# Gate and up products of a SwiGLU layer: k-tiles outside and both token tiles inside, in place of one token tile after the other

## Chip, cores, metric

One core of one Trainium2 chip. The metric is the device time of one launch in microseconds (us). The kernel before takes 947.87 us, the median of 3 runs (947.01 to 948.15). TensorE is called PE below, VectorE DVE, ScalarE ACT, GpSimd POOL, SyncE SP.

## What is computed

A two-layer encoder over 256 tokens of width 1024, all in float32. Each layer is a feed-forward half step, a mixer and a second feed-forward half step, each of them behind an RMSNorm:

```
def swiglu(h, w_gate, w_up, w_down):
    return (jax.nn.silu(h @ w_gate) * (h @ w_up)) @ w_down

for layer in range(DEPTH):                       # DEPTH = 2
    x = x + 0.5 * swiglu(rms_norm(x, ffn1_norm[layer]), ...)
    x = x + mixer(rms_norm(x, mix_norm[layer]))  # attention; even and odd layers differ
    x = x + 0.5 * swiglu(rms_norm(x, ffn2_norm[layer]), ...)
return rms_norm(x, final_norm)
```

The four feed-forward steps (width 2816) are the stages 0, 2, 3 and 5 of the kernel; the mixers are stages 1 and 4. The change touches the four feed-forward stages.

## The kernel before

**A product.** Weights come from memory as float32 into tiles `raw` (SP issues the transfers). Each is split in two: `hi`, which ACT copies in a rounded format (L476), and `lo`, the rest, which DVE subtracts (L479). The method `mm` (L459) makes one 128 x 512 product out of three matmuls (L468 to L470): `h*hi`, `h*lo`, `l*hi`, where (h, l) are the two parts of the transposed activations (`th`, `tl`). A piece is one k-tile of 128 rows; a split has two of them, and each piece is used by two products, one for each of the two token tiles (`tt` 0 and 1).

**What sets the order.** The order of every engine's instructions is the order in which the Python code writes them. After every product `mm` calls `tick` (L273). A tick counts down the waits of small tasks (Python generators that write the next ACT or DVE instruction when their wait is over) and adds `self.rate` to a budget `due`. When the budget and `room` (seven `hi`/`lo` pairs may live, L286) allow it, the next split is written. A split that a product needs and that isn't there is written on the spot. All engines then run their rows strictly in this order, and a row that waits holds up everything behind it on its engine.

**Chunks.** `ffn` (L656) goes through five chunks of 512 columns, numbered 0 to 4, and one mixed chunk of 256. There are two kinds. A plain chunk takes 8 gate pieces and 8 up pieces. Gate: `project` (L599) makes all 8 products of token tile 0 in one PSUM bank, then all 8 of token tile 1 in another; behind each a task `silu` (L667) is started, which reads the bank on ACT. Up: the same again, with a task `glu` (L671) behind each, which reads the up bank on DVE (L674) and multiplies. Six ticks later `transposed` (L677) begins: ACT splits the result in two 16-bit planes (L553), SP issues a transposing transfer (L555), and 16 ticks later ACT puts the planes together again (L557) and ACT and DVE split the outcome (`g_h`, `g_l`), or make sums of it (`quarters`).

The other kind, `seven_gates` (L753), makes gate and up of a chunk with seven products in place of eight. It is chunk 2 in stages 0 and 5, and chunks 1 and 3 in stages 2 and 3: six in all. It begins with 8 plain products (16 where two pairs of k-tiles are plain) into the banks M00, M10, M01, M11, with token tiles 0 and 1 in turn; then the seven-product part begins in the banks M1, M5, M7 and M6. At its end ACT copies M1 (`copy`, L764, written `glu<-pj`), DVE reads M00 together with that copy (L785, `silu<-s`), and further DVE rows read M1's companions: L800 reads M01, L804 M10, L806 M5.

**Banks.** PSUM has eight: two with the tag `pj`, three with `s`, one `o`, two `tp` (L126). A tag's banks are given out in turn, and the first matmul into a bank waits until the last reader of what was there before has ended. A plain chunk takes `s, s` for gate and `pj, pj` for up; behind a seven-product chunk it takes `pj, s` for gate and `s, pj` for up (L861). So the first gate bank behind a seven-product chunk is M1's, the second one M00's; the second up bank is M5's. M1, the first `pj` bank of a seven-product chunk, is the one that the chunk before gave to up of token tile 0, where that chunk took `pj, pj` for up; in chunk 3 of stages 2 and 3 it is M01 that takes over the bank of up of token tile 0, an `s` bank there.

## Time and profile before

| what | before |
|---|---|
| time, median of 3 runs | 947.87 us |
| profiled execution: its time | 949.13 us |
| profiled execution: span from first to last instruction | 947.3 us |
| PE busy | 924.9 us, 98% of the span, 4399 matmuls |
| DVE busy | 789.6 us, 83% |
| ACT busy | 678.6 us, 72% |
| POOL busy | 90.8 us, 10% |
| transfers | 183.16 MB, mean 193 GB/s |
| mean granted TensorE clock | 0.996 |

PE is busy in nearly every slice of the profile. Busy isn't the same as at its peak: a matmul of 128 x 512 is shown with some 0.39 us, while the next one begins 0.23 us after it. So what PE loses is read from the distance between the starts of two matmuls, and from idle time in the view of the waits. DVE and ACT make the splits that PE uses, and read the banks that PE fills.

### The profile page before, as it was taken

The page shows a single profiled execution, that of the slowest core. Times are in us where ns is not written, and L with a number is a line of the kernel's source. Part 1 is how long each engine was busy: PE and PEld are TensorE (multiplying, and loading weights), DVE is VectorE, ACT ScalarE, POOL GpSimd, SP SyncE. Part 2 cuts the span into 40 slices and gives each one's busy share as a digit, 9 for nine tenths or more (in the row PEclk, how much of TensorE's full clock was granted, in tenths as well). Part 3 has the DMA queues.
Part 4 walks back from the last instruction along what each step waited for, and adds up shares of the span by engine and source line. Part 5 has one row for each costly group of instructions (what it writes and reads, how often), then busy time and mean ns, then how long its engine had stood idle before and what let it go on. Part 6 is the DMA issues. An engine that isn't in the chain of part 4 may idle for free.

```text
span 947.3 us, 12407 instructions
## 1 busy us (share of the span) xinstructions
PE 924.9 (98%) x4399; PEld 755.3 (80%) x4399; DVE 789.6 (83%) x1228; ACT 678.6 (72%) x1091; POOL 90.8 (10%) x152
## 2 busy tenths in 40 slices
PE   9999999999999999999999999899999999999997
PEld 6887888877788788888888778688778788878886
DVE  6799788778879988798878887988777787988797
ACT  7687875568787687874757868647777587769753
POOL 1300000064410000000100000007030000000001
PEclk9999999999999999999999999999999999999999
DMA  8858986554236677867458677665444449489761
GB/s 297 274 170 243 248 226 215 176 155 102 93 110 189 214 213 230 264 192 266 148 151 250 173 256 208 219 221 159 147 134 134 134 151 271 116 275 256 186 222 45
DMA packets 129343, 183.16 MB, mean 193 GB/s; under 512 B 50688, under 2 KB 63744, under 8 KB 129280
## 3 DMA queue, kind: packets, MB, share of 16 engines
q1 hardware_dynamic: 128704, 181.58, 62.4%
q8 instruction: 34, 0.56, 0.2%
q10 hardware_dynamic: 576, 0.79, 0.2%
q14 instruction: 29, 0.24, 0.1%
HBM read 169.76 MB, written 1.05 MB: 180 GB/s over the span
## 4 chain that ended last, share of the span: by engine, by line
PE 72%; DVE 15%; ACT 6%; issue 4%; DMA 2%; POOL 0%; SPq 0%; POOLq 0%; ACTq 0%; DVEq 0%
PE s L469 10%; PE s L470 10%; PE s L468 10%; PE pj L468 9%; PE pj L469 9%; PE pj L470 9%; DVE lo L479 6%; PE o L470 2%; PE o L469 2%; PE o L468 2%; ACT hi L476 2%; PE o L1038 2%; DVE raw L394 1%; DVE two L394 1%; PE tp L1117 1%
## 5 line engine op out<-in xcount | busy, mean ns | idle before, releaser
L479 DVE TENSOR_TENSOR lo<-raw,hi 128x1024 fp32r<-128x1024 f32 (+1 forms) x372 | 376.2, 1030 | 83.6 <-ACT hi L476 81.9
L476 ACT ACTIVATE hi<-raw 128x1024 fp32r<-128x1024 f32 (+1 forms) x372 | 319.3, 889 | 54.5 <-PE s L470 16.7
L469 PE MATMUL s<-lo,th 128*128 128x512 f32 x373 | 145.9, 391 | 2.5 <-DVE lo L479 2.4
L468 PE MATMUL pj<-hi,th 128*128 128x512 f32 x367 | 146.6, 399 | 1.3 <-ACT glu L764 1.3
L468 PE MATMUL s<-hi,th 128*128 128x512 f32 x373 | 146.2, 392 | 0.0
L470 PE MATMUL s<-hi,tl 128*128 128x512 f32 x373 | 145.6, 390 | 0.0
L469 PE MATMUL pj<-lo,th 128*128 128x512 f32 x367 | 143.5, 391 | 1.6 <-DVE lo L479 1.5
L470 PE MATMUL pj<-hi,tl 128*128 128x512 f32 x367 | 143.2, 390 | 0.0
L469 PEld LDWEIGHTS s<-lo,th 128*128 128x128 f32 x373 | 70.2, 188 | 18.2 <-DVE lo L479 4.0
L469 PEld LDWEIGHTS pj<-lo,th 128*128 128x128 f32 x367 | 69.1, 188 | 16.0 <-DVE lo L479 3.3
L470 PEld LDWEIGHTS s<-hi,tl 128*128 128x128 f32 x373 | 70.2, 188 | 14.5
L468 PEld LDWEIGHTS s<-hi,th 128*128 128x128 f32 x373 | 70.1, 188 | 14.2
L468 PEld LDWEIGHTS pj<-hi,th 128*128 128x128 f32 x367 | 69.0, 188 | 15.6 <-ACT glu L764 1.7
L470 PEld LDWEIGHTS pj<-hi,tl 128*128 128x128 f32 x367 | 68.9, 188 | 14.5
L488 POOL TENSOR_TENSOR rstd<-var,mhalf 128x1 f32<-128x1 f32 (+2 forms) x16 | 17.1, 1070 | 601.8 <-ACT th L509 321.5
L557 ACT COPY turned<-glu 128x1024 uint16<-128x1024 uint16 (+1 forms) x48 | 60.2, 1254 | 6.1 <-DMA glu<-turned 6.1
L470 PE MATMUL s<-hi,g_l 128*128 128x512 f32 (+1 forms) x131 | 51.5, 393 | 3.6 <-DVE g_l L479 3.6
L553 ACT COPY turned<-glu 128x1024 uint16<-128x1024 uint16 (+1 forms) x48 | 46.2, 963 | 8.9 <-DVE glu L674 6.7
L468 PE MATMUL s<-hi,g_h 128*128 128x512 f32 (+1 forms) x131 | 52.0, 397 | 0.0
L469 PE MATMUL s<-lo,g_h 128*128 128x512 f32 (+1 forms) x131 | 51.3, 392 | 0.0
L476 ACT ACTIVATE shi<-two 128x1024 fp32r<-128x1024 f32 x30 | 31.7, 1057 | 26.2 <-DVE two L394 26.1
L476 ACT ACTIVATE shi<-raw 128x1024 fp32r<-128x1024 f32 x30 | 31.7, 1056 | 23.9 <-PE s L470 13.0
(483 smaller groups left out, 1685.3 us busy)
## 6 DMA issues: line engine op xcount, KB each, us to landing
raw<-in_ffn_w_down SPq DMA_DIRECT2D x44, 1024.0 KB, 5.4
raw<-in_ffn_w_up SPq DMA_DIRECT2D x28, 1024.0 KB, 5.3
raw<-in_ffn_w_gate SPq DMA_DIRECT2D x26, 1024.0 KB, 5.2
raw<-in_ffn_w_gate SPq DMA_DIRECT2D x35, 512.0 KB, 4.1
raw<-in_ffn_w_up SPq DMA_DIRECT2D x32, 512.0 KB, 5.2
raw<-in_odd_w_qkv SPq DMA_DIRECT2D x12, 1024.0 KB, 5.4
raw<-in_even_w_in SPq DMA_DIRECT2D x4, 1024.0 KB, 5.1
raw<-in_even_w_out SPq DMA_DIRECT2D x8, 512.0 KB, 5.7
```

The costliest lines, as they stand in the source:

```text
L394: add = lambda o, x, y: self.nc.vector.tensor_tensor(o, x, y, op=ALU.add)
L468: mm(ps, h, wh, start=first, stop=False)
L469: mm(ps, h, wl, start=False, stop=False)
L470: mm(ps, l, wh, start=False, stop=last)
L476: self.nc.scalar.activation(hi, src, AF.Copy)
L479: self.nc.vector.tensor_tensor(lo, src, hi.bitcast(F32), op=ALU.subtract)
L488: nc.gpsimd.tensor_tensor(r[:, :n], v[:, :n], self.mhalf[:, :n], op=ALU.pow)
L553: self.nc.scalar.copy(planes.rearrange("p (h c) -> p h c", h=2), back.rearrange("p (c h) -> p h c", h=2))
L557: self.nc.scalar.copy(planes.rearrange("p (c h) -> p h c", h=2), back.rearrange("p (h c) -> p h c", h=2))
L1038: self.nc.tensor.matmul(O[64 * s : 64 * s + 64, i * P : i * P + P], v(b0 + i, s, kc), pT[s][:, i, kc, :], start=(kc == 0), stop=(kc == 1),)
L1117: nc.tensor.transpose(tb[:, o : o + P], p[:, i, kc * P : kc * P + P], self.ident)
```

## The change

```
     def project(self, hT, pieces, tag):
...
+    def project_both(self, pieces, tags):
+        ps = [self.bank(tag) for tag in tags]
+        n = len(pieces)
+        for k in range(n):
+            for tt in range(NT):
+                self.mm(ps[tt], self.now.hT[tt][k], pieces[k], k == 0, k == n - 1)
+        return ps
...
             if self.now.n + ci == 0:
                 both = self.first_gates(G)
+            if ci:
+                both = self.project_both(G, tags[:NT])
             for tt in range(NT):
-                g = both[tt] if self.now.n + ci == 0 else self.project(self.ready(tt), G, tags[tt])
+                g = both[tt] if self.now.n + ci == 0 or ci else self.project(self.ready(tt), G, tags[tt])
                 S.append(self.t([P, 512], "silu", 2))
                 self.start(silu(tt, w, g, S[tt]))
             U = self.take(KD)
+            last = ci + 1 == len(FF_CHUNKS)
+            if not last:
+                both = self.project_both(U, tags[NT:])
             for tt in range(NT):
-                u = self.project(self.now.hT[tt], U, tags[NT + tt])
+                u = self.project(self.now.hT[tt], U, tags[NT + tt]) if last else both[tt]
                 tasks.append(self.start(glu(tt, f0, w, u, S[tt])))
```

Gate of the plain chunks from chunk 1 on (10 of them) and up of all plain chunks but chunk 4 (10 too, and chunk 0 among them) now take each piece for both token tiles in turn. The number of products and of ticks is the same. Both banks are in use from the first two products on, and both `silu`, or both `glu`, are started behind the sixteenth product; before, the first was started behind the eighth. A piece is first used later (but for the first one) and is done with sooner.

Three places show what moved. The names end in numbers that count the tiles; between the two kernels they differ by a few.

The first is PE at the start of chunk 4 of stage 2, behind a seven-product chunk. Here `pj_3760` is the bank of gate for token tile 0 (`th_2918` its activations), and `s_3761` that for token tile 1 (`th_3004`). Before:

```order
L468 MATMUL pj_3760<-hi_3697,th_2918 128x512
L469 MATMUL pj_3760<-lo_3698,th_2918 128x512
L470 MATMUL pj_3760<-hi_3697,tl_2919 128x512
L468 MATMUL pj_3760<-hi_3697,th_2918 128x512
L469 MATMUL pj_3760<-lo_3698,th_2918 128x512
L470 MATMUL pj_3760<-hi_3697,tl_2919 128x512
```

And with the change:

```order
L468 MATMUL pj_3760<-hi_3690,th_2918 128x512
L469 MATMUL pj_3760<-lo_3691,th_2918 128x512
L470 MATMUL pj_3760<-hi_3690,tl_2919 128x512
L468 MATMUL s_3761<-hi_3690,th_3004 128x512
L469 MATMUL s_3761<-lo_3691,th_3004 128x512
L470 MATMUL s_3761<-hi_3690,tl_3005 128x512
```

The bank of token tile 1 is taken at the fourth matmul of the chunk; before, it was taken at the twenty-fifth.

The second is ACT at the same place, in the last part of the seven-product chunk 3 of stage 2. `turned` are results of up of chunk 2 (two token tiles); `glu<-pj` is the copy of M1. Before:

```order
L553 COPY turned_3628<-glu_3581 128x1024
L476 ACTIVATE shi_3630<-two_3610 128x1024
L557 COPY turned_3568<-glu_3525 128x2x512
L698 ACTIVATE quarters_3670<-turned_3568 128x256
L476 ACTIVATE g_8_h_3672<-turned_3568 128x512
L476 ACTIVATE shi_3688<-raw_3481 128x1024
L476 ACTIVATE hi_3697<-raw_3537 128x1024
L476 ACTIVATE hi_3704<-raw_3537 128x1024
L557 COPY turned_3628<-glu_3581 128x2x512
L701 ACTIVATE quarters_3670<-turned_3628 128x128
L764 ACTIVATE glu_3718<-pj_3663 128x512
L476 ACTIVATE hi_3720<-raw_3600 128x1024
```

And with the change:

```order
L476 ACTIVATE shi_3681<-raw_3479 128x1024
L476 ACTIVATE hi_3690<-raw_3520 128x1024
L476 ACTIVATE hi_3697<-raw_3520 128x1024
L557 COPY turned_3629<-glu_3580 128x2x512
L557 COPY turned_3631<-glu_3582 128x2x512
L706 ACTIVATE quarters_3711<-turned_3629 128x256
L476 ACTIVATE g_8_h_3713<-turned_3629 128x512
L709 ACTIVATE quarters_3711<-turned_3631 128x128
L772 ACTIVATE glu_3717<-pj_3662 128x512
L476 ACTIVATE hi_3719<-raw_3591 128x1024
```

The three rows of token tile 0 (`COPY turned`, `quarters`, `g_8_h`) stood ahead of the last `shi`; now they stand behind it and behind two `hi`, right ahead of the copy of M1.

The third is DVE at the end of chunk 2 of stage 2, where up ends and the seven-product chunk begins. `glu<-s` reads the up bank of token tile 0, `glu<-pj` that of token tile 1. Before:

```order
L674 SCALAR_TENSOR_TENSOR glu_3525<-s_3488,rstd_2940,silu_3437 128x512
L479 TENSOR_TENSOR lo_3531<-raw_3409,hi_3530 128x1024
L479 TENSOR_TENSOR lo_3547<-raw_3455,hi_3546 128x512
L394 TENSOR_TENSOR two_3553<-raw_3455 128x1024
L394 TENSOR_TENSOR raw_3455<-two_3553,raw_3455 128x512
L394 TENSOR_TENSOR raw_3455<-raw_3455 128x512
L479 TENSOR_TENSOR g_4_l_3544<-turned_3446,g_4_h_3543 128x512
L479 TENSOR_TENSOR lo_3562<-raw_3455,hi_3561 128x1024
L674 SCALAR_TENSOR_TENSOR glu_3581<-pj_3521,rstd_3030,silu_3487 128x512
L479 TENSOR_TENSOR slo_3584<-two_3553,shi_3583 128x1024
```

And with the change:

```order
L479 TENSOR_TENSOR lo_3514<-raw_3410,hi_3513 128x1024
L479 TENSOR_TENSOR lo_3529<-raw_3445,hi_3528 128x512
L394 TENSOR_TENSOR two_3535<-raw_3445 128x1024
L394 TENSOR_TENSOR raw_3445<-two_3535,raw_3445 128x512
L394 TENSOR_TENSOR raw_3445<-raw_3445 128x512
L479 TENSOR_TENSOR lo_3553<-raw_3445,hi_3552 128x1024
L479 TENSOR_TENSOR g_4_l_3550<-turned_3451,g_4_h_3549 128x512
L479 TENSOR_TENSOR slo_3561<-two_3535,shi_3560 128x1024
L682 SCALAR_TENSOR_TENSOR glu_3580<-s_3487,rstd_2940,silu_3485 128x512
L682 SCALAR_TENSOR_TENSOR glu_3582<-pj_3488,rstd_3030,silu_3486 128x512
```

The reader of the first up bank went from the head of these rows to their end, and one `slo` more stands ahead of it.

## Prediction

> **What bounds the kernel now.** The busy times come first, then PE's waits.

> ```profile
> PE 924.9 (98%) x4399; PEld 755.3 (80%) x4399; DVE 789.6 (83%) x1228; ACT 678.6 (72%) x1091; POOL 90.8 (10%) x152
> ```

> ```profile
> PE s L470 <- DVE g_l L479: 3.6, 1, 3.6
> PE s L469 <- DVE lo L479: 2.4, 2, 2.0
> PE pj L469 <- DVE lo L479: 1.5, 2, 0.9
> ```

> PE is the bound: it idles 22.4 of 947.3 us, and its longest sum of waits for one thing is 3.6. So little can be won, and whatever makes PE wait once more is paid in full. The question is whether the new order makes it wait, and for whom.

> **What the change takes away.** A plain chunk before needs its four splits within 8 products; with the change within 16, so splits 2 to 4 are first used 6, 12 and 18 matmuls later. Where PE waited for a late `lo` of such a chunk, that wait goes: the third wait row above, 1.5 us, is the fourth split of gate in chunk 3 of stages 0 and 5. This one, in chunk 4 of stage 2, is of the same kind:

> ```profile
> 369.50 0.39 PE L468 MATMUL pj<-hi,th 128*128 128x512 f32 x1
> 369.87 0.50 PE L469 MATMUL pj<-lo,th 128*128 128x512 f32 x1
> ```

> The starts lie 0.37 us apart where 0.23 is usual. With a like one at the start of stage 0 and the slow restart behind each, I put all of this at **-2.5 us**. Matmuls, splits, transfers and their bytes are the same in number, so nothing else goes away.

> **What it adds: banks that are read late.** The second gate bank behind a seven-product chunk is M00's, and DVE's L785 reads it. Chunk 4 of stage 2, PE, then ACT, then DVE:

> ```profile
> 365.42 0.39 PE L468 MATMUL pj<-hi,th 128*128 128x512 f32 x1
> ...
> 366.10 0.39 PE L468 MATMUL pj<-hi,th 128*128 128x512 f32 x1
> ...
> 371.14 0.39 PE L468 MATMUL s<-hi,th 128*128 128x512 f32 x1
> ```

> ```profile
> 355.86 1.34 ACT L557 COPY turned<-glu 128x1024 uint16<-128x1024 uint16 x1
> 357.23 0.42 ACT L698 ACTIVATE quarters<-turned 128x256 f32<-128x256 f32 x1
> 357.55 0.62 ACT L476 ACTIVATE g_h<-turned 128x512 fp32r<-128x512 f32 x1
> 359.50 1.06 ACT L476 ACTIVATE shi<-raw 128x1024 fp32r<-128x1024 f32 x1 [1.33 <-PE pj L470]
> ...
> 363.97 0.58 ACT L764 ACTIVATE glu<-pj 128x512 f32<-128x512 f32 x1
> 364.45 1.05 ACT L476 ACTIVATE hi<-raw 128x1024 fp32r<-128x1024 f32 x1
> ```

> ```profile
> 365.53 1.23 DVE L479 TENSOR_TENSOR lo<-raw,hi 128x1024 fp32r<-128x1024 f32 x1 [1.43 <-ACT hi L476]
> 366.67 0.42 DVE L704 TENSOR_TENSOR quarters<-turned,quarters 128x256 f32<-128x256 f32 x1
> 367.00 0.69 DVE L785 TENSOR_TENSOR silu<-s,glu 128x512 f32<-128x512 f32 x1
> ```

> L785 ends at 367.69. Before, the second bank is wanted at 371.14, and nobody sees it. With the change it is wanted at 366.10, the fourth matmul of the chunk: 1.6 us short as it stands. And L785 comes later. ACT's three rows from 355.86 to 358.17 go behind the two `hi` after 359.50 and ahead of the copy of M1; the `shi` at 359.50 waits for PE, so ACT can't begin it sooner, and the gap of 1.33 us that they leave stays empty. So the copy of M1 ends 2.3 us later (366.9, past the gate's start at 365.42), the `hi` behind it too, and DVE, which waits for that `hi` already, with it. One `g_l` (0.6) also comes to stand ahead of L785. L785 then ends at 367.69 + 2.3 + 0.6 = 370.6, and PE loses 370.6 - 366.10 = **4.5 us**. The product that waits has all later ones of PE behind it.

> The same for the other five. L785 runs six times:

> ```profile
> L785 DVE TENSOR_TENSOR silu<-s,glu x6: 684/685/687, 73.5 to 829.0; 128x512 f32<-128x512 f32 x6
> ```

> ```profile
> 73.38 0.39 PE L468 MATMUL pj<-hi,th 128*128 128x512 f32 x1
> ...
> 828.84 0.39 PE L468 MATMUL pj<-hi,th 128*128 128x512 f32 x1
> ```

> The first ends at 74.2, 0.8 us behind the fourth matmul; the last at 829.7, 0.9 behind. In stage 3 it is 2.2 (chunk 2) and 2.3 (chunk 4); in stage 2, chunk 2, it ends 1.2 us in time. The moved ACT rows (2.0 us in stage 3, chunk 2, where there are no `quarters`) and the `g_l` come on top in chunk 2 of stage 3: 4.8. In chunk 4 of stage 3 ACT was late ahead of them, so its own copy of M1 keeps its time and only the `g_l` is added: 2.9. In stage 5 ACT stood idle long enough: 0.9. In stage 0 PE is already held up more than this by the next term: 0. Sum **13.1 us**, bounds 7.0 (2.2 + 2.3 + 1.6 + 0.9, ACT's delay hidden) and 15.

> **The reader of the first up bank.** Both `glu` now stand behind the sixteenth product of up. The bank of the first is wanted at once: as M01, the third product of the next chunk, in stages 2 and 3 (chunk 3), and as M1, the ninth, in stages 0 and 5. Chunk 3 of stage 2 (PE's third product, and DVE):

> ```profile
> 346.38 0.39 PE L468 MATMUL s<-hi,th 128*128 128x512 f32 x1
> ```

> ```profile
> 342.30 1.23 DVE L479 TENSOR_TENSOR lo<-raw,hi 128x1024 fp32r<-128x1024 f32 x1 [0.68 <-ACT hi L476]
> 345.18 0.69 DVE L479 TENSOR_TENSOR lo<-raw,hi 128x512 fp32r<-128x512 f32 x1 [1.66 <-ACT hi L476]
> ...
> 350.11 0.74 DVE L674 SCALAR_TENSOR_TENSOR glu<-pj,rstd,silu 128x512 f32<-128x512 f32 x1
> 350.77 1.22 DVE L479 TENSOR_TENSOR slo<-two,shi 128x1024 fp32r<-128x1024 f32 x1
> ```

> In the new order the first `glu` stands behind the `slo` that ends at 351.99; the two `glu` that were ahead of that leave (2 x 0.66), and it adds its own 0.66: 351.3. If the earlier splits let DVE fill its two idle gaps (0.68 + 1.66), 349.0. Against 346.38 that is 2.6 to 4.9 us; I take 3.4, nearer the first, since the splits are written 12 to 15 matmuls sooner. Chunk 3 of stage 3 by the same rows is 4.2 to 6.9, less some 3 by which PE comes later than DVE from the chunk before: 2.0 (1.2 to 3.9). Stage 0 (PE's M1, and DVE):

> ```profile
> 57.83 0.39 PE L468 MATMUL pj<-hi,th 128*128 128x512 f32 x1
> ```

> ```profile
> 59.97 0.74 DVE L674 SCALAR_TENSOR_TENSOR glu<-pj,rstd,silu 128x512 f32<-128x512 f32 x1
> 60.63 1.22 DVE L479 TENSOR_TENSOR lo<-raw,hi 128x1024 fp32r<-128x1024 f32 x1
> 61.76 1.22 DVE L479 TENSOR_TENSOR slo<-two,shi 128x1024 fp32r<-128x1024 f32 x1
> ```

> The first `glu` comes behind both splits: 62.98 less 0.66 is 62.3, and 61.3 if DVE starts a us sooner; 3.5 to 4.5 behind 57.83; I take 3.5. In stage 5 the same sum ends within PE's time (0, up to 1.9). Sum **8.9 us** (7.3 to 15).

> **Two smaller ones.** The second up bank behind a seven-product chunk is M5's, read by L806; with DVE set back as above it is late in stages 0 and 5: **3 us** (0 to 8). And in chunk 1 of stage 2 both `COPY turned` now stand together ahead of a `shi` that had one of them ahead: PE waits there for DVE already, so **1.5 us** (0 to 3).

> **The restart.** Behind a long wait PE's steps are longer for a while (stage 2, chunk 1):

> ```profile
> 317.69 0.80 PE L469 MATMUL s<-lo,th 128*128 128x512 f32 x1 [1.96 <-DVE lo L479]
> ...
> 321.21 0.40 PE L468 MATMUL pj<-shi,k16h 128*128 128x512 f32 x1
> ```

> Eight matmuls take 3.52 us there, and 8 x 0.23 = 1.84 is usual: 1.7 lost behind a wait of 1.96. Of the new waits six or seven are of 2 us or more. I count four restarts that are paid in full, since a slower PE also shortens the wait that follows (DVE goes on meanwhile): **6.8 us** (0 to 12). [...]

> **Sum.** -2.5 + 13.1 + 8.9 + 3 + 1.5 + 6.8 = +30.8 us. The durations are of an execution of 949.13 us (947.3 of span and what lies around it), which becomes 979.9; this execution was 1.3 us above the median of the runs, so the median becomes 947.87 + 30.8 = **979 us**. All terms at their lower ends: -2.5 + 7.0 + 7.3 = 11.8, so 960. At their upper: -2.5 + 15 + 15 + 8 + 3 + 12 = 50.5, so 998.

> **Rivals.**
> - *The late readers, and hardly more*: DVE fills its gaps and ACT's three moved rows are hidden. Then the lower ends hold, some 12 to 18 us: 960 to 966, say 963. For it speaks that the splits are written 3 to 18 matmuls sooner around each seven-product chunk, so that DVE can work ahead; against it, that ACT's `shi` rows wait for PE (the 359.50 row), so ACT's gaps can't be moved. Chance 0.2.
> - *A worse pile-up*: a second `COPY turned` (L557) comes to wait for a transfer, since both of a chunk are now issued together, and all ACT rows behind it wait too. ACT waits for these transfers for little now; at 4 us more in six places, with what follows from it, 1005. Chance 0.08.
> - *Faster*: DVE gets so far ahead that the readers are in time. Its place is L785 in chunk 4 of stage 2, and it decides from the point at which that row ends before 366.10, that is 1.6 us sooner than now and 4.5 sooner than I reckon. Then no bank is waited for, the -2.5 is left, and half of PE's waits for `lo` in the seven-product chunks may go with it (2.4 us in the second wait row): 944. For it speaks DVE's idle time before the 345.18 row; against it, that L785's wait is for an ACT row, which waits for PE. Chance 0.05.
> - *No difference*: the two orders give PE the same matmuls, and all waits balance: 948. It would need the second bank to be free in each of the six places, and five of six miss it already. Chance 0.04.

> **How the numbers follow.** The forecast, 966 to 998 around 979, has 0.63. With 0.2 for the case below it, a range of 957 to 996 leaves out the worse pile-up, the two cases at and below 948, and a little of the top of the forecast: 2 in 10. A measurement of this kernel tells 0.2%, about 2 us, from no change. Faster by more than that 0.05, within it 0.04, slower by more 0.91.

> **What would show it right or wrong.** In the profile after, PE's waits should be headed by rows of `pj` and `s` at L468 that wait for DVE's L785, L674 and L806 and ACT's L764 (at their new lines, 8 to 14 further down), with 4 us or so each in chunk 4 of stage 2, chunk 2 of stage 3 and at the start of chunk 3 of stage 2, and PE idle some 45 us in all. The waits for `lo` in the first gates behind a seven-product chunk should be gone. DVE's and ACT's busy times should be as they are. The forecast is wrong if PE's waits for these readers sum to less than 10 us; it is wrong in its largest term if L785 ends no later, seen from the gate's first matmul, than now.

## The result, and the profile after

The changed kernel takes 982.21 us, the median of 4 runs (980.46 to 984.60), beside 948.01 (947.01 to 950.14) for the kernel before: a ratio of 1.0357, 95% interval 1.0339 to 1.0375. It is 34 us slower. The forecast was 979 us, 3 us less, and the measured time lies well inside its range. The profiled execution took 983.87 us.

The profile after, first its span and granted clock, then the busy times:

```profile
core 0: 982.1 us, clock 0.977
```

```profile
PE 940.0 (96%) x4399; PEld 764.5 (78%) x4399; DVE 790.8 (81%) x1228; ACT 677.8 (69%) x1091; POOL 94.5 (10%) x152
```

The same 4399 matmuls are done. PE idles 982.1 - 940.0 = 42.1 us in place of 22.4, which is 19.7 more, and it is busy 15.1 us longer for the same work. So the 34.8 us of the span have two parts: waits, and matmuls that run slower. DVE and ACT are busy as before, within 1.2 us. PE's waits (us in total, times, longest):

```profile
PE s L468 <- DVE silu L793: 8.6, 3, 3.0
PE pj L468 <- DVE silu L814: 4.6, 2, 2.7
PE pj L468 <- ACT glu L772: 3.9, 5, 0.9
PE pj L468 <- DVE glu L682: 3.6, 2, 3.0
PE s L468 <- DVE glu L682: 3.6, 2, 2.8
PE s L470 <- DVE g_l L479: 2.6, 1, 2.6
PE s L469 <- DVE lo L479: 2.2, 2, 2.0
```

The first five are waits for a bank that is still to be read; lines stand 8 further down than before (L785 is L793, L674 is L682, L806 is L814, L764 is L772). They sum to 24.3 us. Before, one row of the kind stood in the list, 1.3 us for the copy of M1:

```profile
PE pj L468 <- ACT glu L764: 1.3, 1, 1.3
```

Chunk 4 of stage 2, the place of which the prediction said most, in the chain of waits from 377 us on (start, length, what):

```profile
377.36 2.46 ACT turned L557 x2
379.82 0.27 ACT quarters L706
380.10 0.52 ACT g_h L476
380.61 0.20 ACT quarters L709
380.81 0.48 ACT glu L772
381.29 0.96 ACT hi L476
382.25 0.02 issue
382.27 1.23 DVE lo L479
383.50 0.60 DVE g_l L479
384.10 0.34 DVE quarters L712
384.44 0.61 DVE silu L793
385.05 0.04 issue
385.09 0.80 PE s L468
```

Read it downwards: both `COPY turned` and `g_h` stand ahead of the copy of M1, which PE's first gate product waits for; then one `hi`, its `lo`, a `g_l`, a `quarters`, and only then L793, the reader of M00, for which PE's fourth matmul waits until 385.09. ACT could not start this sooner, because a `shi` stood in front and waited for PE:

```profile
374.41 1.06 ACT L476 ACTIVATE shi<-raw 128x1024 fp32r<-128x1024 f32 x1 [7.66 <-PE pj L470]
```

The second part shows in the stretch behind that wait (busy us of PE, PEld, DVE, ACT and POOL, then the granted clock, DMA share and GB/s):

```profile
384.70:390.60 5.90, 5.51 (x13) 4.35 (x14) 5.87 (x9) 5.14 (x6) 0.00 (x0) 0.51 0.40 123
390.60:396.50 5.90, 5.90 (x27) 4.84 (x27) 5.76 (x10) 3.40 (x4) 0.00 (x0) 1.00 0.70 235
```

For 5.9 us PE has half its clock: 13 matmuls in place of 27. The other new bank waits of 1.9 us or more, seven in all, are followed by such a stretch too.

### The profile page after: what moved, and what is told of

Its sections match the earlier page's. It is cut to its first block, busy times and chain, and to the rows that moved or that the text cites. A ratio compares the mean times of both kernels' runs of the same rounds, so it can differ in the third digit from the quotient of the medians.

```text
span 982.1 us, 12430 instructions
## 1 busy us (share of the span) xinstructions
PE 940.0 (96%) x4399; PEld 764.5 (78%) x4399; DVE 790.8 (81%) x1228; ACT 677.8 (69%) x1091; POOL 94.5 (10%) x152
## 3 DMA queue, kind: packets, MB, share of 16 engines
HBM read 169.76 MB, written 1.05 MB: 174 GB/s over the span
## 4 chain that ended last, share of the span: by engine, by line
PE 72%; DVE 13%; ACT 8%; issue 5%; DMA 1%; POOL 0%; POOLq 0%; ACTq 0%; DVEq 0%
PE s L468 10%; PE s L470 10%; PE s L469 10%; PE pj L468 10%; PE pj L470 9%; PE pj L469 9%; DVE lo L479 5%; ACT hi L476 3%; ACT turned L557 2%; PE o L470 2%; PE o L469 2%; PE o L468 2%; PE o L1051 2%; DVE two L394 1%; PE tp L1130 1%
## 5 line engine op out<-in xcount | busy, mean ns | idle before, releaser
L479 DVE TENSOR_TENSOR lo<-raw,hi 128x1024 fp32r<-128x1024 f32 (+1 forms) x372 | 376.0, 1029 | 80.7 <-ACT hi L476 79.5
L476 ACT ACTIVATE hi<-raw 128x1024 fp32r<-128x1024 f32 (+1 forms) x372 | 320.1, 890 | 76.3 <-PE s L470 33.5
L468 PE MATMUL s<-hi,th 128*128 128x512 f32 x373 | 149.7, 401 | 12.7 <-DVE silu L793 8.6
L468 PE MATMUL pj<-hi,th 128*128 128x512 f32 x367 | 149.9, 408 | 12.1 <-DVE silu L814 4.6
L469 PE MATMUL s<-lo,th 128*128 128x512 f32 x373 | 148.4, 398 | 2.2 <-DVE lo L479 2.2
L470 PE MATMUL s<-hi,tl 128*128 128x512 f32 x373 | 148.2, 397 | 0.0
L470 PE MATMUL pj<-hi,tl 128*128 128x512 f32 x367 | 145.1, 395 | 0.0
L469 PE MATMUL pj<-lo,th 128*128 128x512 f32 x367 | 145.1, 395 | 0.0
L468 PEld LDWEIGHTS s<-hi,th 128*128 128x128 f32 x373 | 71.6, 192 | 30.4 <-DVE silu L793 10.3
L468 PEld LDWEIGHTS pj<-hi,th 128*128 128x128 f32 x367 | 70.5, 192 | 29.9 <-ACT glu L772 6.0
L469 PEld LDWEIGHTS s<-lo,th 128*128 128x128 f32 x373 | 71.6, 192 | 18.0 <-DVE lo L479 3.4
L470 PEld LDWEIGHTS s<-hi,tl 128*128 128x128 f32 x373 | 71.6, 192 | 15.2
L470 PEld LDWEIGHTS pj<-hi,tl 128*128 128x128 f32 x367 | 70.1, 191 | 15.3
L469 PEld LDWEIGHTS pj<-lo,th 128*128 128x128 f32 x367 | 70.5, 192 | 13.0
L479 DVE TENSOR_TENSOR slo<-raw,shi 128x1024 fp32r<-128x1024 f32 x30 | 36.6, 1222 | 36.5 <-ACT shi L476 36.5
L553 ACT COPY turned<-glu 128x1024 uint16<-128x1024 uint16 (+1 forms) x48 | 45.5, 967 | 28.3 <-DVE glu L799 17.5
L476 ACT ACTIVATE shi<-raw 128x1024 fp32r<-128x1024 f32 x30 | 31.7, 1056 | 40.3 <-PE pj L470 18.0
L557 ACT COPY turned<-glu 128x1024 uint16<-128x1024 uint16 (+1 forms) x48 | 58.6, 1249 | 0.5 <-DMA glu<-turned 0.4
L470 PE MATMUL s<-hi,g_l 128*128 128x512 f32 (+1 forms) x131 | 51.6, 394 | 2.6 <-DVE g_l L479 2.6
L468 PE MATMUL s<-hi,g_h 128*128 128x512 f32 (+1 forms) x131 | 51.7, 394 | 0.0
L469 PE MATMUL s<-lo,g_h 128*128 128x512 f32 (+1 forms) x131 | 51.3, 391 | 0.0
```

The costliest lines, as they stand in the source:

```text
L468: mm(ps, h, wh, start=first, stop=False)
L469: mm(ps, h, wl, start=False, stop=False)
L470: mm(ps, l, wh, start=False, stop=last)
L476: self.nc.scalar.activation(hi, src, AF.Copy)
L479: self.nc.vector.tensor_tensor(lo, src, hi.bitcast(F32), op=ALU.subtract)
L553: self.nc.scalar.copy(planes.rearrange("p (h c) -> p h c", h=2), back.rearrange("p (c h) -> p h c", h=2))
```

## The experiments

Each edit is shown against the changed kernel where nothing else is said. Ratios are to the kernel before.

**Gate alone.**

```
             U = self.take(KD)
-            last = ci + 1 == len(FF_CHUNKS)
+            last = True
```

> Only gate takes both token tiles inside; up is as before the change. Theory (late bank readers, made later still by the rows that up moves): DVE's reader of M00 is late by what it was late before, 2.2 + 2.3 + 1.6 + 0.9 = 7.0 us over the four places, with two or three slow restarts of 1.9 us (5), less 2.5 for the waits for lo that go: about +9.5, 957 us, and no wait for the glu or M5 readers. Rival A (the gate order alone makes those waits, the rows that up moves do not matter): the 12.5 us of L793 and L772 waits and three restarts stay, less 2.5: about 964. Rival B (all of the loss comes from up): 946 to 948.

It takes 953.07 us, ratio 1.0037 (1.0023 to 1.0050), some 4 us less than expected. PE's waits:

```profile
PE s L468 <- DVE silu L793: 7.5, 6, 2.2
...
PE pj L468 <- ACT glu L772: 0.9, 1, 0.9
...
PE pj L468 <- DVE glu L682: 0.4, 1, 0.4
```

The wait for M00's reader is 7.5 us: what the rows of before gave with nothing moved on ACT (7.0, and 0.8 for chunk 3 of stage 0, which the prediction had hidden behind another wait). So rival A falls, and rival B too, since the gate alone does cost waits. The time is below the expectation in the main because the waits are short ones, 2.2 at most: only two of them are followed by half clock, in stage 3 (3.5 us by the steps between matmul starts over 0.227 us, where I had counted 5), and the slow stretch of 1.7 us that the kernel before has in chunk 1 of stage 2 is missing here. The other 3.0 us of L772 and 1.1 of L793 in the change come from what up moves. (In chunk 4 of stage 2 and chunks 2 and 4 of stage 3 the waits for L793 are 2.9 us longer in the change; the three short ones of 0.3 to 0.8 us in stages 0, 2 and 5 are not there.)

**Up alone.**

```
-            if ci:
+            wide = False
+            if wide:
                 both = self.project_both(G, tags[:NT])
...
-                g = both[tt] if self.now.n + ci == 0 or ci else self.project(self.ready(tt), G, tags[tt])
+                g = both[tt] if self.now.n + ci == 0 or wide else self.project(self.ready(tt), G, tags[tt])
```

> Only up takes both token tiles inside; gate is as before the change. Theory: the waits for the glu reader (7.2 us) and the M5 reader (4.6 us) stay with their four restarts (2.5 + 1.7 + 1.7 + 1.7 = 7.6), the waits for the M00 reader go, since token tile 1's bank is wanted 24 matmuls into the gate: about +19, 967 us. So gate alone and up alone sum to about 28 of the 34 us of the change, and the rest is what each adds to the other. Rival (the parts are independent): this run and the gate run sum to 34 within 2. Rival (up's readers are late only because the gate order has set DVE back): under +8, below 956.

It takes 975.76 us, ratio 1.0288 (1.0270 to 1.0306): +27, not +19. The two parts sum to 31 us by the ratios and 32 by the medians, between the theory's 28 and the rival's 34, so the sum doesn't tell the two apart. PE's waits do, since they are not those of the change less the gate's:

```profile
PE s L468 <- DVE glu L682: 9.7, 2, 5.1
PE pj L469 <- DVE lo L479: 5.0, 5, 1.5
PE pj L468 <- ACT glu L772: 4.0, 5, 0.9
...
PE pj L468 <- DVE glu L682: 3.4, 2, 2.8
```

The waits for the first up bank's reader are 13.1 us here and 7.2 in the change; in chunk 3 of stage 3 alone 5.1 here and 0.8 there:

```profile
548.02 0.79 PE L468 MATMUL s<-hi,th 128*128 128x512 f32 x1 [5.12 <-DVE glu L682]
```

With the gate order of before, PE isn't held at the gate of the chunk ahead, so it comes to this bank sooner and waits here instead. M5's reader, 4.6 us in the change, isn't waited for in this run nor in the one before: it takes both orders to set DVE back so far. And the copy of M1 is waited for 4.0 us with gate as before: its delay is up's doing. The first gates wait 5.0 us for a late `lo`, where they waited 1.5 before. In all PE idles 42.5 us, as much as in the change (42.1). What the change has more is half clock: PE is busy 8.9 us longer than before here, and 15.1 us in the change.

**Away from the seven-product chunks.** The new order in 6 blocks of 20.

```
-            if ci:
+            wide = ci and ci - 1 not in sevens
+            if wide:
                 both = self.project_both(G, tags[:NT])
...
-            last = ci + 1 == len(FF_CHUNKS)
+            last = ci + 1 == len(FF_CHUNKS) or ci - 1 in sevens or ci + 1 in sevens
```

> The new order only in the blocks that touch no seven-product chunk: gate of chunks 1 and 4 and up of chunk 0 in stages 0 and 5 (6 of the 20 blocks). Theory: no bank is read late there, the order itself costs PE nothing: 947 to 949 us. Rival (taking the two token tiles in turn costs PE something in every block, such as a change of bank and of activations at each product): 34 us / 20 blocks x 6 = +10, 958 us.

It takes 947.84 us, ratio 0.9988 (0.9977 to 0.9998). The order itself costs PE nothing in these blocks; its rival, 10 us, falls. All of the loss stands at the borders of the seven-product chunks.

**Padding the seven long waits.** A method `pad` makes matmuls with a tile of zeros (`none`) as one operand into a bank that is open anyway, 60 in all. They wait for nobody and change no value. In `PAD` the place is given by stage, chunk and product, then comes the number of matmuls; the two places of `PAD_SEVEN`, in the plain products of a seven-product chunk, get 9 each.

```
+    def pad(self, ps, n):
+        moving = self.hts[self.now.n, 0][0][:, 0:4, :].rearrange("p k t -> p (k t)")
+        for _ in range(n):
+            self.nc.tensor.matmul(ps, self.none, moving, start=False, stop=False, skip_group_check=True)
...
                 self.mm(ps[tt], self.now.hT[tt][k], pieces[k], k == 0, k == n - 1)
+                if k == tt == 0:
+                    self.pad(ps[0], pad)
...
+PAD = {(0, 3, "up"): 6, (2, 4, "gate"): 9, (3, 2, "gate"): 9, (3, 4, "gate"): 9, (5, 3, "up"): 9}
+PAD_SEVEN = [(0, 2, 1, 1, 0), (2, 3, 0, 0, 0)]
```

> The change, with 6 to 9 matmuls that add zero to a bank that is open anyway, put ahead of each of the seven long new waits, so that PE idles there under 1 us; every other row as in the change. Theory (each long idle time is followed by a stretch at half clock that is paid in full): the seven stretches (2.5 + 1.7 + 1.7 + 2.2 + 1.7 + 2.4 + 1.7 = 13.9 us) go: about 968 us, clock back to 0.99. Rival of the prediction (a slower PE shortens the wait that follows, so only about half is paid): 974 to 976. Rival (the slow stretches have another cause than idle time): 982, with the stretches still there.

It takes 970.16 us, ratio 1.0224 (1.0207 to 1.0242), 12 us less than the change. The same place in chunk 4 of stage 2:

```profile
376.40 2.21 PE L621 MATMUL pj<-th,none 128*128 128x512 f32 x9
379.34 0.50 PE L470 MATMUL s<-hi,th 128*128 128x512 f32 x1 [0.73 <-DVE silu L802]
379.68 0.39 PE L471 MATMUL s<-lo,th 128*128 128x512 f32 x1
379.90 0.40 PE L472 MATMUL s<-hi,tl 128*128 128x512 f32 x1
```

The padded bank comes no sooner (nine steps of 0.23 and a wait of 0.73 are the 2.78 that the change waits here), but behind it the matmuls come every 0.23 us at once. The mean clock of this run is 0.995. So idle time is the cause of the half clock, and nearly all of it is paid: of the 13.9 us that were counted, 12 come back. The rival with half of it falls. The profiles agree: the 60 matmuls take 13.6 us at 0.227, and without them PE is busy 14.2 us less than in the change; its idle time and these matmuls together are 0.9 us more than the idle time of the change.

**A lag between the token tiles.** Token tile 1 runs LAG pieces behind token tile 0, and `silu` or `glu` is started behind a token tile's own last product (`then`). With 8 the order is that of before, with 0 nearly that of the change.

```
-        for k in range(n):
+        for step in range(n + LAG):
             for tt in range(NT):
-                self.mm(ps[tt], self.now.hT[tt][k], pieces[k], k == 0, k == n - 1)
-        return ps
+                k = step - tt * LAG
+                if 0 <= k < n:
+                    self.mm(ps[tt], self.now.hT[tt][k], pieces[k], k == 0, k == n - 1)
+                    if k == n - 1:
+                        then(tt, ps[tt])
```

> The change with token tile 1 running 2 pieces behind token tile 0 in every changed block (0 is the change, 8 is the order of before); silu or glu of a token tile is started behind its own last product. Theory (a bank wanted sooner than its reader is done, and a restart behind each wait over some 1.9 us): the second bank is wanted 6 matmuls = 1.36 us later and the first up reader is written 2 pieces sooner, so the long waits of 2.8 to 3.0 fall to about 1.5, the waits for L793, L682 and L814 from 20.4 to about 9.5, and with them all seven restarts (13.9) go, since none is left over 1.9: 982 - 11 - 14 = 957 us. Rival (loss in proportion to the lag, no threshold): 982 - 34 x 2/8 = 973.5 us.

> The same with token tile 1 running 4 pieces behind. Theory: the second bank is wanted 12 matmuls = 2.7 us later, so no wait for L793, L682 or L814 over 0.5 us is left; what remains of the ACT copy's waits (L772, 3.9 in the change) is 1 to 3 us, and the waits for a late lo in the first gates (1.5) go: 947 to 950 us. Rival (in proportion): 965 us.

Lag 2 takes 953.08 us, ratio 1.0043 (1.0028 to 1.0057); lag 4 takes 948.87, ratio 0.9991 (0.9978 to 1.0003). In proportion it would have been 973.5 and 965. Lag 2 does better than the 957 expected, lag 4 lies inside its range. With a quarter of the way back, nearly nine tenths of the loss is gone. A lag does two things, it takes the second bank later and starts the first reader sooner; they were not tried apart. The waits of lag 2, then of lag 4:

```profile
PE s L469 <- DVE glu L686: 3.0, 2, 2.3
PE pj L469 <- ACT glu L776: 3.0, 2, 1.5
PE s L469 <- DVE silu L797: 2.7, 3, 1.1
...
PE pj L469 <- DVE silu L818: 0.3, 1, 0.3
```

```profile
PE pj L469 <- ACT glu L776: 3.1, 3, 1.3
...
PE pj L469 <- DVE glu L686: 0.3, 1, 0.3
```

At lag 2 the readers cost 9.0 us of waits (L776 is the copy of M1, L797 reads M00, L686 the first up bank, L818 M5), and of these only the wait of 2.3 us is still followed by half clock. At lag 4, but for 0.3 us, only the copy of M1 is left.

**Padding the kernel before.** The same `pad`, against the kernel before, at its two waits that had a slow stretch behind them:

```
+                if (self.now.n, ci, q) == (2, 1, KD // 2 - 1):
+                    self.pad(M["00"], 6)
                 product("00", h[0][k], b21, q == 0, last)
...
                         use(f, tt, slice(half * 512, half * 512 + 512))
+                    if (self.now.n, f, tt) == (3, 20, 0):
+                        self.pad(Y[0][1], 11)
```

> The kernel before, with 6 matmuls that add zero ahead of the wait of 1.96 us in chunk 1 of stage 2 and 11 ahead of the wait of 3.65 us in stage 3's down part; every other row as before. Theory (idle time of about 2 us and more brings the half clock, and padding keeps it away): both slow stretches (1.3 and 1.6 us) go and nothing else changes: -2.9, 945 us, ratio 0.997. Rival (a slow PE costs nothing there, since the wait behind it is shorter by as much): 948.

It takes 946.91 us beside 949.68 for the kernel before in the same runs, ratio 0.9969 (0.9957 to 0.9981): faster by the 2.9 us expected (1.8 to 4.1 by the interval). Not everything else stayed as it was: the profiled execution, of 947.09 us, has both stretches gone, but a new slow one at 544 us behind a wait of 1.27 us, and a wait of 1.79 us at 663 us where the kernel before has 0.55.

**Two versions to beat both.** The first puts that padding into the kernel of the 6 blocks.

> The new order in the 6 blocks away from the seven-product chunks, and the two paddings of the kernel before (6 and 11 matmuls that add zero). Theory: the two gains add, 0.9988 x 0.9969 = 0.9957, 944 to 945 us. Rival (they take away the same thing, or the padding's gain needs the old order): no better than the padding alone, 0.997.

945.22 us, ratio 0.9965 (0.9951 to 0.9978). This can't be told from the padding alone (0.9969), nor from the 0.9957 of the theory; whether the 0.12% of the 6 blocks adds stays open.

The second has lag 4 for the gates, up in the new order in chunk 0 of stages 0 and 5 alone (with lag 4 too), and three paddings, the third being

```
+                if (self.now.n, ci, q) == (3, 3, KD // 2 - 1):
+                    self.pad(M["10"], 5)
                 product("6", K[1][j], t6, first, last)
```

> Gate of all ten plain chunks with token tile 1 four pieces behind, up so in chunk 0 of stages 0 and 5 alone, the two paddings of the kernel before, and 5 matmuls that add zero behind the sixth product at the end of chunk 3 of stage 3, where three waits of 0.4, 0.8 and 1.3 us lie within 5 us. Theory: no bank is read late, the first gates wait no more for lo (-1.5), and up has moved no rows in front of the copy of M1 (its wait stays at 1.3): 0.995 to 0.996, 943 to 945 us. Rival (the copy's waits rise to 3 us as with lag 4 in both): 0.998.

943.96 us beside 948.67, ratio 0.9950 (0.9938 to 0.9963). It is the fastest of the study. PE's longest waits:

```profile
PE s L470 <- DVE lo L480: 2.0, 5, 0.6
PE o L1519 <- DVE zeros L1513: 1.4, 1, 1.4
PE s L471 <- DVE g_l L480: 1.2, 1, 1.2
```

No bank reader is among them. It is faster than the version before it in the same runs (943.58 to 944.28 against 944.87 to 945.59); against the padding alone, 0.9957 to 0.9981 in other runs, the intervals touch. How much of the gain over the padding alone is the gate's lag, and how much the third padding, was not tried apart.

## Why the prediction was right, and where it was off

| step | forecast, us | found, us | from |
|---|---|---|---|
| waits for a late `lo` that go | -2.5 | -1.5 | the row of 1.5 is gone; no half clock stood behind these short waits |
| second gate bank (L793, with ACT's L772) | +13.1 | +11.2 | 8.6 + 3.9 - 1.3 |
| reader of the first up bank (L682) | +8.9 | +7.2 | 3.6 + 3.6 |
| second up bank (L814) | +3 | +4.6 | 4.6 |
| pile-up in chunk 1 of stage 2 | +1.5 | +0.9 | new waits of 0.17 and 0.76; that of 1.96 us is as before |
| slow restarts | +6.8 | +15.1 | PE busy, 940.0 - 924.9 |
| not foreseen: the `g_l` of stage 3 | 0 | -1.0 | 3.6 before, 2.6 after |
| not foreseen: `shi` and `slo` in chunk 3 of stage 3 | 0 | -1.2 | waits of 0.44 and 0.77, gone |
| sum | +30.8 | +35.3 | the span: +34.8 |

The pile-up in the change:

```profile
322.29 0.50 PE L468 MATMUL s<-shi,th 128*128 128x512 f32 x1 [0.17 <-ACT shi L476]
323.55 0.50 PE L469 MATMUL s<-slo,th 128*128 128x512 f32 x1 [0.76 <-DVE slo L479]
```

**The mechanism was right.** The waits are headed by the readers that were named, with PE idle 42.1 us where 45 were said. The second gate bank fits place by place: for 4.5, 4.8, 2.9, 0.9 and 0 us (chunk 4 of stage 2, chunks 2 and 4 of stage 3, stages 5 and 0) PE lost 3.6, 4.0, 2.4, 0.7 and 0.6. Gate alone shows the first part of the second-gate-bank step by itself: readers that were late all along, but whom nobody waited for. Up alone and gate alone together show its second part, the rows that up pushes in front of the copy of M1.

**The mis-sized term is the slow restart.** The prediction took four at 1.7 us, since "a slower PE also shortens the wait that follows". Seven came, and they cost 2.2 us each on the mean (15.1 / 7). Against the padded run the rebate is small: 12 us come back when the clock is kept up, and PE waits about 1 us more. Most of this 1 us stands in chunk 3 of stage 3, where the wait for L682's row is 1.57 us in the padded run and 0.82 in the change. The next bank wait lies a chunk or more further on, and the reader there is released by PE's own progress, over ACT's `shi`: a slower PE makes that reader late by as much. This last sentence is argued from the 7.66 us row; no run tested it apart. That the time came within 3 us of the forecast is in part luck: the waits were reckoned 4 us too long in sum (24.0 for 20.2), the restarts 8 us too short (6.8 for 15.1).

**The step of chunk 3 in stage 3 was right in its reason and too long.** It said 4.2 to 6.9 us "less some 3 by which PE comes later than DVE from the chunk before". Without that delay, in up alone, the wait is 5.1. In the change it is 0.8, below the 1.2 to 3.9 that were left:

```profile
551.86 0.50 PE L468 MATMUL s<-hi,th 128*128 128x512 f32 x1 [0.82 <-DVE glu L682]
```

**The rival of the worse pile-up failed at its root.** ACT's wait of the second `COPY turned` for transfers did not grow; it went from 6.1 us before to 0.5 (the costliest groups; the last numbers are idle time and what ended it):

```profile
L557 ACT COPY turned<-glu 128x1024 uint16<-128x1024 uint16 (+1 forms) x48 | 60.2, 1254 | 6.1 <-DMA glu<-turned 6.1
```

```profile
L557 ACT COPY turned<-glu 128x1024 uint16<-128x1024 uint16 (+1 forms) x48 | 58.6, 1249 | 0.5 <-DMA glu<-turned 0.4
```

The rows stand later in ACT's order, so their transfers have long landed. The rival "late readers, and hardly more" (963) had DVE working ahead, for 12 to 18 us in all; the bank waits alone are 24.3 us. *Faster* had its point at L785 ending 1.6 us sooner; it ends later, 3.7 us behind the start of the gate's first matmul (385.03 less 381.34) where it was 2.3. *No difference* falls by the 34 us.

**My forecast for up alone was too low** (967 for 975.76). I carried over 7.2 us of waits for the first up bank and 4.6 for M5's reader; they were 13.1 and 0. Left out were 2.7 us more for the copy of M1 and 3.5 more for `lo` in the first gates, and PE's longer busy time is 8.9 where 7.6 was said: +8.8 us together. The trade with the gate's waits was in the prediction's own working for stage 3. In stage 2 the wait grew from 2.8 to 4.6 us. There the change has a slow stretch of 1.6 us in chunk 1 that this run's profiled execution lacks; PE reaches the bank 3.1 us sooner without it (1.5 of this it had already ahead of the stretch), the reader ends 1.2 sooner. So here a slow stretch seems to have shortened the next wait by about its length, as the prediction had it; no run tested this apart.

## What to carry to other kernels

Before two accumulations are interleaved, look up who last reads the bank of the second one and when: an order that takes one bank after the other can hide a late reader for 24 matmuls, and the interleaved one for 3. Between both extremes lies a lag, and a lag of half the length cost nothing here (948.87 us, ratio 0.9991). Here a new wait of about 2 us came to nearly twice its length where PE's clock fell behind it (1.96 us of wait and 1.7 us at half clock in the kernel before; the clock fell when PE idled 1.86 us or more within one stretch of 3.41): count it so where the profile shows the fall, and fill a wait that can't be removed with matmuls that add zero (60 of them brought 12 us back here).

## What the runs showed of the hardware

```profile
314.30:317.71 3.41, 1.45 (x8) 1.00 0.92 297
317.71:321.13 3.42, 3.42 (x8) 0.50 0.11 17
```

```profile
312.95:316.37 3.42, 2.28 (x10) 1.00 0.70 204
316.37:319.78 3.41, 2.56 (x11) 1.00 0.27 103
```

In the kernel before the whole wait lies in one stretch, PE idles 1.96 us of it, and the next one has half clock. In the 6 blocks the wait is cut in two, 1.14 and 0.85 us, and the clock stays. The same was found throughout: in the eleven profiled executions 26 periods of half clock begin between the first rise of the clock and 930 us. Ahead of each stands a stretch in which PE idles 1.86 us or more, and no other stretch at full clock has more than 1.79 us. Short waits added up as well: in the padded kernel of before a wait of 1.27 us was followed by half clock, and it and most of one of 0.77 us lie in one stretch. In the change nine waits were followed by half clock, the seven new ones among them; the shortest of the nine is 1.86 us, the longest 3.05.

**The slow stretches of the change cost about 1.7 or about 2.8 us each**, so the 1.7 that the prediction read from one row was the smaller of two sizes. In the change four of the seven new ones lie at 1.6 to 1.8 and three at 2.6 to 2.9, by the same count of steps. The four have half clock for 3.41 us, the three for 6.83. The long ones came where the wait goes on into the slow stretch, as in chunk 4 of stage 2:

```profile
380.22:383.63 3.41, 1.23 (x5) 1.00 1.05 399
383.63:387.04 3.41, 1.95 (x5) 0.50 0.07 23
387.04:390.46 3.42, 3.42 (x10) 0.50 0.63 193
```

Of the 26 periods 7 are long; in these PE still idles 0.80 us or more in the first 3.41 us at half clock, in the 19 short ones 0.49 us or less.
